# A decoder layer on one core: the third MLP weight block's cast and the four residual scalings are queued behind the last conversions of the MLP's input

## The chip, the cores and the metric

One core of one Trainium2 chip runs the kernel as a single program. The metric is the time of one execution on the device in microseconds (us). Engines are named as in the profile: PE is the tensor engine (PEld its weight loads), ACT the scalar engine, DVE the vector engine, POOL the GpSimd engine, and SP the engine whose queue issues most loads. All weights and activations are float32.

## The reference, cut to what matters

The layer mixes tokens by two branches (causal pooling and a state-space scan), merges them through gates and `w_o`, and then runs a squared-ReLU MLP. The part around the change is the end of the mixing and the start of the MLP:

```python
h = h + (gate_pool * y_pool + gate_ssd * y_ssd) @ w_o[i]
v = rmsnorm(h, mlp_norm_w[i])            # the kernel does this for the 512 tokens that are kept
hid = jax.nn.relu(v @ w_ff1[i])          # 1024 -> 4096
h = h + (hid * hid) @ w_ff2[i]           # 4096 -> 1024
out = rmsnorm(h, final_norm_w)           # the 16 meta tokens are dropped
```

## The kernel before, in words

Each float32 operand of a product is split into a high half, rounded to the type float32r (`vh`, `whi`, `hh`), and a low half, which is the rest (`vl`, `wlo`, `hl`). A product is then three PE products: high by high, low by high, high by low. ACT makes the high half by a cast, and DVE makes the low half by a subtraction that needs the high half. So each weight block of 128x1024 costs a load, one ACT cast and one DVE subtraction, and PE waits for both.

**Weights.** `block()` takes a block's tiles, loads `raw` over SP's queue (`block_load`, L85) and splits it (`block_split`: the cast on L93, the subtraction on L95). There are three `raw` buffers, used in turn: the load of a block waits until the block three places earlier has been cast and subtracted. `whi` and `wlo` have four buffers each. In this stretch the blocks are, by the numbers that the built program gives them: `raw_6687` and `raw_6728` (MLP columns 0 and 1), `raw_6810` and `raw_6843` (columns 2 and 3, the second pair), `raw_6885` and `raw_6918` (columns 4 and 5), `raw_7025` and `raw_7094` (columns 6 and 7). `raw_6918` takes the buffer of `raw_6810`. SP's queue also loads quarters of `w_ff2` and sums of them (`quarter`, L1195: tiles `b` and `t`). POOL loads and stores such sums through a queue of its own at the same time.

**The MLP's input.** The residual `ht` has four tiles of 128 tokens by 1024 channels. PE transposes it in four pieces (`turn`, L1085) into the PSUM banks `ptA`, `ptB`, `ptC` and `ptD`; `turned` (L1089 to L1100) makes from each piece four `vh` on ACT (L1094) and four `vl` on DVE (L1095), and from `ptA` and `ptD` also four plain copies `vf` on ACT (L1099). `ptD` is the last piece. The norm's factor is not applied to `v`: squares of `ht` are summed on ACT (L1077) into `ssum`, DVE makes `m2` from it (L1392 and L1393), and ACT multiplies the four tiles of `ht` by `m2` (L1397), so that all is in the same scale when the MLP's output is added.

**The MLP.** `ff1_plain(n)` multiplies two blocks (columns 2n and 2n+1) with `vh` and `vl` into PSUM banks `pf`, and ACT applies ReLU and the square (L1217 and L1218). For a pair of columns, `left_factors` (L1331 to L1349) makes the operands of the second product, which runs as Strassen-like products of sums of quarters: ACT casts `hh` (L1338 for three segments, L1348 for the other four), DVE subtracts `hl` (L1339, L1349) and makes the sums (L1344 to L1347). `sums_of_v` makes sums of quarters of `v` for later first products (DVE L1263 to L1275, ACT L1274). The second products accumulate in the PSUM tile `alpha` (`prod`, L1359 and L1362); after each, DVE adds it to `ht` (`onto`, L1066), and the next product accumulates into the same `alpha`, so it waits until that addition has read it.

**The order.** Each engine has a queue of its own and works in the order of its queue; an instruction that waits for a semaphore holds all behind it on its engine. The order on each engine comes from a scheduler, which the program may bind with `tc.issue_after(x)`: what is issued inside stands behind `x` on `x`'s engine. Pools of buffers and PSUM banks give the other dependences.

Of the kernel before, what the change touches and what calls it, by code (L numbers as in the profile page):

```python
# [11 lines left out]
AF = mybir.ActivationFunctionType  # L12
# [22 lines left out]
V_MIX, V_BG, V_PS, V_CW, V_CB, V_DS, V_SN, V_MN, V_DTB, V_AL = (  # L35
    0, 8, 24, 32, 160, 192, 208, 224, 232, 233)
# [27 lines left out]
def kernel(ctx: ExitStack, tc, xT, x, w, f1, f2, vec, fnw, out):  # L64
    nc = tc.nc
    act, dve, pe, pool = nc.scalar, nc.vector, nc.tensor, nc.gpsimd
# [10 lines left out]
    def block_tiles():  # L77
        b = nblk[0]
        nblk[0] += 1
        return (b, wp.tile([P, 1024], F32, tag="raw", name=f"raw{b}", bufs=3),  # L80
                wp.tile([P, 1024], F32R, tag="whi", name=f"whi{b}"),
                wp.tile([P, 1024], F32R, tag="wlo", name=f"wlo{b}"))

    def block_load(t, c):
        nc.sync.dma_start(t[1][:, c], w[t[0], :, c])  # L85

    def block_part(t, c):
        block_load(t, c)
        block_split(t, c)

    def block_split(t, c, behind=None):
        b, raw, hi, lo = t
        act.copy(hi[:, c], raw[:, c])  # L93
        with tc.issue_after(behind.ins) if behind is not None else nullcontext():
            dve.tensor_tensor(lo[:, c], raw[:, c], hi[:, c].bitcast(F32), op=ALU.subtract)  # L95

    def block(behind=None):
        t = block_tiles()
        block_load(t, slice(0, 1024))
        block_split(t, slice(0, 1024), behind)  # L100
        return t[2:]
# [48 lines left out]
    def col(off, i, n=P):  # L150
        return vs[:n, off + i : off + i + 1]
# [21 lines left out]
    def psum1(name):  # L173
        return psb.tile([P, 512], F32, tag="s", name=name)
# [151 lines left out]
    for i in range(2):  # L326
        pb = psum1(f"pb1_{i}")
        c = slice(3 * i, 3 * i + 3)
# [35 lines left out]
    for c in (slice(0, P), slice(P, W)):  # L364
        n = c.stop - c.start
# [634 lines left out]
    first = []  # L1000
    for n, d in enumerate(MERGE):
# [10 lines left out]
        wh, wl = block()  # L1012
# [13 lines left out]
    ht = hp_.tile([P, 4, D], F32, name="ht")  # L1026
# [14 lines left out]
    vh = [yp.tile([P, SEQ], F32R, tag="yh", name=f"vh{k}") for k in range(NK)]  # L1041
# [32 lines left out]
    def square_sums(T, half):  # L1074
        cs = slice(half * 512, (half + 1) * 512)
        for t in (2 * T, 2 * T + 1):
            act.activation(junk, ht[:, t, cs], AF.Square, accum_out=ssum[:, t, half : half + 1])  # L1077

    def turn(pts, T, half, ts=(0, 1)):

        for kk in range(4):
            k = 4 * half + kk
            for t in ts:
                o = (kk % 2) * 256 + t * P
                pe.transpose(pts[kk // 2][:, o : o + P], ht[:, 2 * T + t, k * P : (k + 1) * P], ident)  # L1085

    low_end = [None]

    def turned(pts, T, half):  # L1089
        for kk in range(4):  # L1090
            k = 4 * half + kk
            src = pts[kk // 2][:, (kk % 2) * 256 : (kk % 2) * 256 + 256]
            o = slice(256 * T, 256 * T + 256)
            act.activation(vh[k][:, o], src, AF.Copy, scale=col(V_MN, k))  # L1094
            low_end[0] = dve.scalar_tensor_tensor(vl[k][:, o], src, col(V_MN, k), vh[k][:, o].bitcast(F32),  # L1095
                                                  op0=ALU.mult, op1=ALU.subtract)
        for kk in range(0 if half else 4):
            k = 4 * half + kk
            act.activation(v32[k][:, o], pts[kk // 2][:, (kk % 2) * 256 : (kk % 2) * 256 + 256], AF.Copy,  # L1099
                           scale=col(V_MN, k))  # L1100
# [31 lines left out]
    turn(pt, 0, 0)  # L1132
    onto(1, 1, alpha, SUB)
    turned(pt, 0, 0)
    square_sums(0, 0)
    t4 = wo_split("b11")
    wo_prod(q5, "S4", s4, False, True)
    pp = psum2("ptB")
    pt = [pp[:, :512], pp[:, 512:]]
    turn(pt, 1, 1)  # L1140
    turned(pt, 1, 1)
    for t in range(2):
        onto(0, 1, q5[t], ADD, t)
    wo_prod(av, "A22", t4, False, True, (0,))
    onto(1, 0, av[0], ADD, 0)
    pt = banks("ptC")
    turn(pt, 0, 1)
    turned(pt, 0, 1)
    second_half = low_end[0]
    wo_prod(av, "A22", t4, False, True, (1,))  # L1150
# [2 lines left out]
    turn(ptD, 1, 0, (0,))  # L1153


    def ff1_begin(c, f):
        wh, wl = block()
        return psum1(f"pf{c}_{f}"), wh, wl

    def ff1_part(p, ks, first, last):  # L1160
        ps, wh, wl = p
        cs = [slice(k * P, (k + 1) * P) for k in ks]
        mm3s(ps, [((wh[:, c], wl[:, c]), (vh[k], vl[k])) for c, k in zip(cs, ks)], first, last)

    pf = [ff1_begin(0, 0)]
    ff1_part(pf[0], range(4, 8), True, False)
    turn(ptD, 1, 0, (1,))
    turned(ptD, 1, 0)
    for q in ((1, 1), (0, 1), (1, 0)):
        square_sums(*q)  # L1170
    pf.append(ff1_begin(0, 1))
    ff1_part(pf[1], range(4, 8), True, False)
    for p in pf:
# [9 lines left out]
    m2 = fa.tile([P, 4], F32, name="m2")  # L1183
# [14 lines left out]
    def pair_tile(n):  # L1198

        return tmp.tile([P, 4, 256], F32, tag="relu", name=f"r{n}")  # L1200
# [3 lines left out]
    def ff1_plain(n, parts=(range(NK),)):  # L1204
        r = pair_tile(n)
        for i in range(2):
            if pf:
                ps = pf.pop(0)[0]
            else:
                p = ff1_begin(n, i)  # L1210
                ps = p[0]
                for ks in parts if i else (range(NK),):
                    ff1_part(p, ks, ks[0] == 0, ks[-1] == NK - 1)
                    if ks[-1] < NK - 1 or not i:
                        yield
            ri = flat4(r[:, 2 * i : 2 * i + 2, :])
            act.activation(ri, ps, AF.Relu)  # L1217
            act.activation(ri, ri, AF.Square)  # L1218
        left_factors(n, r)
        yield  # L1220
# [110 lines left out]
    def left_factors(n, r):  # L1331

        c, p = divmod(n, 2)
        if p == 0:
            hids[c] = [hid.tile([P, 2, 7, 256], F32R, tag=t, name=f"{t}{c}") for t in ("hh", "hl")]
        hh, hl = (t[:, p] for t in hids[c])
        m = 4 if c == NC - 1 else 3
        act.copy(hh[:, :m, :], r[:, :m, :])  # L1338
        dve.tensor_tensor(hl[:, :m, :], r[:, :m, :], hh[:, :m, :].bitcast(F32), op=ALU.subtract)  # L1339
        if c == NC - 1:  # L1340
            return
        q = [r[:, i, :] for i in range(4)]

        dve.tensor_tensor(q[1], q[3], q[1], op=ALU.subtract)  # L1344
        dve.tensor_tensor(q[3], q[2], q[3], op=ALU.subtract)
        dve.tensor_tensor(q[2], q[1], q[2], op=ALU.subtract)
        dve.tensor_tensor(q[0], q[0], q[2], op=ALU.add)  # L1347
        act.copy(hh[:, 3:, :], r)  # L1348
        dve.tensor_tensor(hl[:, 3:, :], r, hh[:, 3:, :].bitcast(F32), op=ALU.subtract)  # L1349
# [39 lines left out]
    for n in range(3):  # L1389
        for _ in ff1_plain(n):  # L1390
            pass
# [2 lines left out]
    dve.tensor_tensor(be, m2, m2, op=ALU.mult)  # L1394
    dve.tensor_scalar(be, be, EPS, None, op0=ALU.mult)
    for t in range(4):
        act.activation(ht[:, t, :], ht[:, t, :], AF.Copy, scale=m2[:, t : t + 1])  # L1397

    sums_of_v(0)

    for c in range(NC - 1):
        z, e = c == 0, c == NC - 2

        n = 2 * c + 3
        a = ff1_plain(n, (range(4), range(4, NK))) if n < PLAIN else ff1_pair(n)
        b = ff1_pair(n + 1) if n + 1 < 16 else iter(())
        slots = [[a] * (1 if n < PLAIN else 2)] * 3 + [[a, b]] + [[b, b]] * 3
# [60 lines left out]
    c = NC - 1  # L1468
# [14 lines left out]
    for t in range(4):  # L1483
        T, st = t // 2, slice((t % 2) * P, (t % 2 + 1) * P)
        n = 0
        for half in range(2):
            parts = [(0, 512)] if half == 0 or t < 3 else [(0, 256), (256, 256)]
            for a, m in parts:
# [3 lines left out]
                i = 0  # L1492
# [4 lines left out]
                for k, seg in ((1, (A11, 3)[T]), (0, (A12, A22)[T])):  # L1497
                    wh, wl = wq[k, half]
                    for p in range(2):
                        x0 = p * 512 + a  # L1500
                        f = i == 0 and not (T == 0 and half == 0) and not a
# [5 lines left out]
                src = ps  # L1507
                if not a:
                    src = ht[:, t, cs]
# [146 lines left out]
```

## Time and profile before

| what | value |
|---|---|
| median of 3 runs | 1003.68 us (1002.7 to 1003.71) |
| the profiled execution, own time | 1003.18 us |
| its span | 1001.4 us |
| granted clock, mean | 0.999 |
| PE busy | 993.2 us (99%) |
| DVE busy | 793.2 us (79%) |
| ACT busy | 602.8 us (60%) |
| loads and stores | 171.47 MB, mean 171 GB/s |

The profiled execution spends 1.78 us outside of its span. Times in the views are microseconds from the span's start. A row of the timeline gives start, duration, engine, line, operation, output and inputs, the shape, how many instructions it merges, and in brackets how long the engine sat idle before it and what ended that. Durations overlap a little at the ends, since an engine begins an instruction while the one before drains.

### The profile page before, as it was taken

The numbers are of one execution on the slowest core, as the hardware profiler recorded it, in microseconds if no ns is written. First come the engines' busy times: TensorE is split into PE (matmuls) and PEld (weight loads), VectorE is DVE, ScalarE is ACT, GpSimd is POOL, SyncE is SP. The second block draws the span as 40 slices with busy tenths as digits, with TensorE's granted clock in tenths as the row PEclk, the third lists the DMA queues.
The fourth block names the chain that finished last, engine by engine and source line by source line (L and its number), as shares of the span: only waits on it lengthen the run. The fifth ranks groups of instructions, "written<-read, shape, count | busy, mean of one in ns | idle before, by whom it ended". The sixth has DMA issues, their size and how long they took to land.

```text
span 1001.4 us, 15539 instructions
## 1 busy us (share of the span) xinstructions
PE 993.2 (99%) x6095; PEld 878.3 (88%) x6095; DVE 793.2 (79%) x1147; ACT 602.8 (60%) x840; POOL 88.1 (9%) x148
## 2 busy tenths in 40 slices
PE   9999999999999999999999999999999999999997
PEld 7889898999889998988998888888889999999986
DVE  7988797979736687979789667876988888888885
ACT  8675958595827439483255343368666656656654
POOL 0022101111002011002201001121100000000000
PEclk9999999999999999999999999999999999999999
DMA  7378763678238635417978632879654464454432
GB/s 242 92 281 226 202 185 117 193 188 234 63 104 253 164 99 160 132 38 213 280 203 234 230 105 71 238 194 303 182 189 148 149 189 149 146 187 150 127 105 85
DMA packets 56202, 171.47 MB, mean 171 GB/s; under 512 B 6400, under 2 KB 7744, under 8 KB 55104
## 3 DMA queue, kind: packets, MB, share of 16 engines
q1 hardware_dynamic: 36576, 105.86, 32.5%
q0 software_dynamic: 18832, 63.71, 24.3%
q8 instruction: 48, 0.79, 0.3%
q10 hardware_dynamic: 720, 0.91, 0.3%
q14 instruction: 26, 0.21, 0.1%
HBM read 161.90 MB, written 48.40 MB: 210 GB/s over the span
## 4 chain that ended last, share of the span: by engine, by line
PE 98%; DMA 1%; ACT 0%; DVE 0%; issue 0%; SPq 0%; ACTq 0%
PE px L191 12%; PE px L1291 8%; PE alpha L1359 6%; PE pz L191 6%; PE px L193 6%; PE px L1294 4%; PE alpha L1362 3%; PE pgp L191 3%; PE pz L193 3%; PE pgs L191 3%; PE py L556 2%; PE pso L127 2%; PE po L550 2%; PE wo_alpha L1053 1%; PE pso L128 1%; PE pso L130 1%
## 5 line engine op out<-in xcount | busy, mean ns | idle before, releaser
L93 ACT CAST whi<-raw 128x1024 fp32r<-128x1024 f32 (+2 forms) x98 | 98.5, 1014 | 105.7 <-PE px L193 33.2
L95 DVE TENSOR_TENSOR wlo<-raw,whi 128x1024 fp32r<-128x1024 f32 (+2 forms) x98 | 114.7, 1176 | 50.9 <-ACT whi L93 33.1
L191 PE MATMUL px<-uh,whi 128*128 128x264 f32 (+1 forms) x448 | 113.2, 291 | 0.0
L193 PE MATMUL px<-ul,whi 128*128 128x264 f32 (+1 forms) x448 | 110.5, 285 | 0.0
L191 PEld LDWEIGHTS px<-uh,whi 128*128 128x128 f32 x448 | 84.6, 189 | 1.8 <-issue 1.4
L193 PEld LDWEIGHTS px<-ul,whi 128*128 128x128 f32 x448 | 84.3, 188 | 0.4 <-issue 0.2
L1066 DVE TENSOR_TENSOR ht<-ht,alpha 128x1024 f32<-128x1024 f32 x35 | 42.7, 1219 | 29.1 <-PE alpha L1359 29.1
L989 ACT CAST shi<-rawf 128x1024 fp32r<-128x1024 f32 x42 | 44.2, 1051 | 28.7 <-PE alpha L1362 18.2
L191 PE MATMUL px<-uh,wlo 128*128 128x264 f32 (+1 forms) x448 | 58.5, 283 | 0.0
L191 PEld LDWEIGHTS px<-uh,wlo 128*128 128x128 f32 x448 | 55.9, 188 | 0.0
L1359 PE MATMUL alpha<-shi,hh 128*128 128x512 f32 x140 | 55.2, 394 | 0.0
L1362 PE MATMUL alpha<-shi,hl 128*128 128x512 f32 x140 | 54.7, 391 | 0.0
L990 DVE TENSOR_TENSOR slo<-rawf,shi 128x1024 fp32r<-128x1024 f32 x42 | 51.2, 1218 | 0.6 <-ACT shi L989 0.6
L1294 PE MATMUL px<-vsl,shi 128*128 128x256 f32 x192 | 47.4, 280 | 0.0
L1291 PE MATMUL px<-vsh,shi 128*128 128x256 f32 x192 | 47.4, 281 | 0.0
L193 PE MATMUL pz<-ul,whi 128*128 128x512 f32 x112 | 43.6, 390 | 0.0
L191 PE MATMUL pz<-uh,whi 128*128 128x512 f32 x112 | 43.6, 389 | 0.0
L577 DVE RECIPROCAL rs<-rs 128x128 f32<-128x128 f32 x32 | 27.2, 909 | 13.9 <-ACT rs L575 13.8
L1359 PE MATMUL alpha<-slo,hh 128*128 128x512 f32 x140 | 37.4, 389 | 0.0
L1291 PEld LDWEIGHTS px<-vsh,shi 128*128 128x128 f32 x192 | 36.2, 188 | 0.9
L1294 PEld LDWEIGHTS px<-vsl,shi 128*128 128x128 f32 x192 | 36.1, 188 | 0.9
L1294 PE MATMUL px<-vl,shi 128*128 128x256 f32 x144 | 36.1, 283 | 0.0
(558 smaller groups left out, 2859.1 us busy)
## 6 DMA issues: line engine op xcount, KB each, us to landing
raw<-in_w SPq DMA_DIRECT2D x104, 512.0 KB, 4.4
f_t<-in_f POOLq DMA_DIRECT2D x38, 512.0 KB, 6.7
f_s<-in_f POOLq DMA_DIRECT2D x26, 512.0 KB, 8.6
b<-in_f SPq DMA_DIRECT2D x21, 512.0 KB, 4.6
rawf<-in_f SPq DMA_DIRECT2D x36, 256.0 KB, 3.2
rawf<-f_t SPq DMA_DIRECT2D x36, 256.0 KB, 3.0
abc<-acs_d POOLq DMA_DIRECT2D x8, 1024.0 KB, 7.6
f_t<-f_t POOLq DMA_DIRECT2D x12, 512.0 KB, 4.4
```

Source lines behind the costliest of these rows:

```text
L93: act.copy(hi[:, c], raw[:, c])
L95: dve.tensor_tensor(lo[:, c], raw[:, c], hi[:, c].bitcast(F32), op=ALU.subtract)
L191: pe.matmul(o, wt, rhs[0][k][:, c], start=part == 0 and k == 0, stop=part == 1 and k == NK - 1)
L193: pe.matmul(o, wt, rhs[1][k][:, c], start=False, stop=False)
L577: dve.reciprocal(rs[:, ctok(c)], rs[:, ctok(c)])
L989: splits.append((act.copy(hi, src), dve.tensor_tensor(lo, src, hi.bitcast(F32), op=ALU.subtract)))
L990: dve.tensor_tensor(lo, src, hi.bitcast(F32), op=ALU.subtract)))
L1066: added[0] = dve.tensor_tensor(o, o, src, op=op)
L1291: pe.matmul(ps, m, f[k][0], start=start and not low and k == 0, stop=stop and low == 1 and k == 3, skip_group_check=True)
L1294: pe.matmul(ps, m, f[k][1], start=False, stop=False, skip_group_check=True)
L1359: pe.matmul(ps[t], hh[:, p, seg, st], m, start=bool(first and not low and p == 0), stop=bool(last and low and p == 1), skip_group_check=True)
L1362: pe.matmul(ps[t], hl[:, p, seg, st], m, start=False, stop=False, skip_group_check=True)
```

## The change

The last `vh` and the last `vl` instruction of the MLP's input are kept as a pair `all_halves`. The third block (columns 2, `raw_6810`, the first of the second pair) has its cast bound behind that last `vh` on ACT and its subtraction behind that last `vl` on DVE. The four scalings of `ht` are bound behind that last `vh` on ACT. Nothing is added or removed, and no data or size changes.

```diff
     def block_split(t, c, behind=None):
         b, raw, hi, lo = t
-        act.copy(hi[:, c], raw[:, c])
+        first, behind = behind if isinstance(behind, tuple) else (None, behind)
+        with tc.issue_after(first.ins) if first is not None else nullcontext():
+            act.copy(hi[:, c], raw[:, c])
...
-            act.activation(vh[k][:, o], src, AF.Copy, scale=col(V_MN, k))
+            high_end[0] = act.activation(vh[k][:, o], src, AF.Copy, scale=col(V_MN, k))
...
-    def ff1_begin(c, f):
-        wh, wl = block()
+    def ff1_begin(c, f, behind=None):
+        wh, wl = block(behind)
...
     turned(ptD, 1, 0)
+    all_halves = (high_end[0], low_end[0])
...
-                p = ff1_begin(n, i)
+
+                p = ff1_begin(n, i, all_halves if (n, i) == (1, 0) else None)
...
     for t in range(4):
-        act.activation(ht[:, t, :], ht[:, t, :], AF.Copy, scale=m2[:, t : t + 1])
+        with tc.issue_after(all_halves[0].ins):
+            act.activation(ht[:, t, :], ht[:, t, :], AF.Copy, scale=m2[:, t : t + 1])
```

The scheduler moves more than these instructions. Line numbers grow by 2 to 5 in the changed kernel. PE's order and POOL's order are the same in both kernels.

ACT's queue before, where the last piece of the input (`ptD`) is converted; `whi_6811` is the cast of the third block, `whi_6844` that of the fourth:

```order
L1094 ACTIVATE vh_6375<-ptB,vs 128x256
L93 CAST whi_6811<-raw_6810 128x1024
L1094 ACTIVATE vh_6375<-ptC_6651,vs 128x256
L93 CAST whi_6844<-raw_6843 128x1024
L1077 ACTIVATE m_3_120,ssum<-ht 128x512
L1094 ACTIVATE vh_6368<-ptD_6681,vs 128x256
L1094 ACTIVATE vh_6370<-ptD_6682,vs 128x256
L1094 ACTIVATE vh_6369<-ptD_6681,vs 128x256
L1094 ACTIVATE vh_6371<-ptD_6682,vs 128x256
L1397 ACTIVATE ht<-ht,m_6787 128x1024
L1099 ACTIVATE vf_6353<-ptD_6681,vs 128x256
```

The same place now:

```order
L1096 ACTIVATE vh_6375<-ptB,vs 128x256
L1096 ACTIVATE vh_6375<-ptC_6651,vs 128x256
L1079 ACTIVATE m_3_120,ssum<-ht 128x512
L1096 ACTIVATE vh_6368<-ptD_6681,vs 128x256
L1096 ACTIVATE vh_6370<-ptD_6682,vs 128x256
L1096 ACTIVATE vh_6369<-ptD_6681,vs 128x256
L1096 ACTIVATE vh_6371<-ptD_6682,vs 128x256
L95 CAST whi_6811<-raw_6810 128x1024
L1101 ACTIVATE vf_6353<-ptD_6681,vs 128x256
```

Both casts have moved behind the four `vh` of `ptD`, the third block's directly behind them and the fourth's behind the four `vf` that follow, and the scalings of `ht` have left this place.

ACT's queue before, some instructions later, where the blocks of columns 4 and 5 are cast (`whi_6886`, `whi_6919`) and the first pair of columns (`r_6794`) becomes `hh_6799`:

```order
L1397 ACTIVATE ht<-ht,m_6787 128x1024
L93 CAST whi_6886<-raw_6885 128x1024
L1217 ACTIVATE r_6794<-pf_0_6693 128x512
L1397 ACTIVATE ht<-ht,m_6787 128x1024
L1218 ACTIVATE r_6794<-r_6794 128x512
L1217 ACTIVATE r_6794<-pf_1_6734 128x512
L93 CAST whi_6919<-raw_6918 128x1024
L1218 ACTIVATE r_6794<-r_6794 128x512
L1397 ACTIVATE ht<-ht,m_6787 128x1024
L1338 CAST hh_6799<-r_6794 128x768
```

The same place now:

```order
L95 CAST whi_6844<-raw_6843 128x1024
L95 CAST whi_6886<-raw_6885 128x1024
L1221 ACTIVATE r_6794<-pf_0_6693 128x512
L1402 ACTIVATE ht<-ht,m_6787 128x1024
L1222 ACTIVATE r_6794<-r_6794 128x512
L95 CAST whi_6919<-raw_6918 128x1024
L1221 ACTIVATE r_6794<-pf_1_6734 128x512
L1402 ACTIVATE ht<-ht,m_6787 128x1024
L1222 ACTIVATE r_6794<-r_6794 128x512
L1402 ACTIVATE ht<-ht,m_6787 128x1024
L1342 CAST hh_6799<-r_6794 128x768
```

Behind the cast of `whi_6919` there stood a square and one scaling ahead of `hh_6799`; now a ReLU, a scaling, a square and another scaling stand there.

SP's queue before, with the loads of the stretch (`raw` blocks of the first product's weights, `b` and `t` of the second's):

```order
L85 DMA raw_6885<-in_w 128x1024
L1195 DMA b_0_6984<-in_f 128x1024
L1195 DMA t_0_7003<-f_t_870 128x1024
L85 DMA raw_6918<-in_w 128x1024
L85 DMA raw_7025<-in_w 128x1024
L1195 DMA b_0_7068<-in_f 128x1024
L1195 DMA b_0_7075<-in_f 128x1024
L85 DMA raw_7094<-in_w 128x1024
```

And now:

```order
L85 DMA raw_6885<-in_w 128x1024
L1198 DMA b_0_6984<-in_f 128x1024
L1198 DMA t_0_7003<-f_t_870 128x1024
L1198 DMA b_0_7068<-in_f 128x1024
L1198 DMA b_0_7075<-in_f 128x1024
L85 DMA raw_6918<-in_w 128x1024
L85 DMA raw_7025<-in_w 128x1024
L85 DMA raw_7094<-in_w 128x1024
```

The two `b` loads, which wait for no `raw` buffer, now stand ahead of the two `raw` loads.

More of the change, by code (lines that the diff above doesn't have):

```diff
@@ L1085, in turn @@
                 pe.transpose(pts[kk // 2][:, o : o + P], ht[:, 2 * T + t, k * P : (k + 1) * P], ident)
-    low_end = [None]
+    low_end, high_end = [None], [None]
     def turned(pts, T, half):
```

## The prediction

> **What bounds the kernel now.** I read the page's head first, then the waits of PE, then the windows of the stretch that the change touches.
>
> ```profile
> span 1001.4 us, 15539 instructions
> PE 993.2 (99%) x6095; PEld 878.3 (88%) x6095; DVE 793.2 (79%) x1147; ACT 602.8 (60%) x840; POOL 88.1 (9%) x148
> PE pdt L233 <- DVE ones_r L138: 1.5, 1, 1.5
> PE px L181 <- DVE xl L241: 0.6, 2, 0.3
> 655.00:720.00 65.00, 65.00 (x303) 53.92 (x302) 53.18 (x85) 49.63 (x85) 11.70 (x17) 1.00 0.88 249
> ```
>
> PE is the bound, and its only two waits, 2.1 us together, are at the start. In the window around the change (columns: PE, PEld, DVE, ACT, POOL, clock, DMA share, GB/s) PE works for 65 of 65 us at full clock. So an earlier conversion of the MLP's input has no PE wait to remove. The change can only cost, by making something late that is now in time; the question is how wide the margins are on ACT, DVE and the loads, which are nearly full here as well.
>
> **The change part by part.** First the conversions themselves and the third block's cast, from the timelines of ACT, DVE and PE.
>
> ```profile
> 673.10 1.08 ACT L93 CAST whi<-raw 128x1024 fp32r<-128x1024 f32 x1
> 677.72 0.82 ACT L1094 ACTIVATE vh<-ptD,vs 128x256 fp32r<-128x256 f32 x2
> 679.56 0.86 ACT L1094 ACTIVATE vh<-ptD,vs 128x256 fp32r<-128x256 f32 x2 [1.02 <-DVE vl L1095]
> 675.00 1.22 DVE L95 TENSOR_TENSOR wlo<-raw,whi 128x1024 fp32r<-128x1024 f32 x1
> 677.22 1.23 DVE L95 TENSOR_TENSOR wlo<-raw,whi 128x1024 fp32r<-128x1024 f32 x1 [1.01 <-ACT whi L93]
> 685.65 0.39 PE L127 MATMUL pf<-vh,whi 128*128 128x512 f32 x1
> ```
>
> The two subtractions at 675.00 and 677.22 leave DVE's way, so the 1.02 us for which ACT waited in the middle of its four `vh` should go. The last `vh` ended at 679.56 + 0.86 = 680.4. It can now end between 677.72 + 0.82 + 0.86 = 679.4 and 680.4; the path to PE gains nothing by it. The third block's cast follows with 1.05 us and its subtraction with 1.22 us: whi at about 681.2, wlo at about 682.0 (bounds 681.7 and 682.7). PE wants that block at 685.65, so the move of the cast itself is covered by 4 us and costs nothing. The fourth block's cast comes behind four `vf` and is wanted a whole product later still: nothing either.
>
> What the move does cost hangs on the buffer. The load of column 5's block (`raw_6918`) takes the third block's buffer, so it waits for that subtraction. SP's timeline, and the time from issue to landing of the loads in it, one by one (t, raw, raw, b, both b, raw):
>
> ```profile
> 673.31 0.33 SPq L1195 DMA_DIRECT2D t<-f_t  x1
> 676.28 2.52 SPq L85 DMA_DIRECT2D raw<-in_w  x2
> 678.85 1.02 SPq L1195 DMA_DIRECT2D b<-in_f  x2
> 686.18 0.33 SPq L85 DMA_DIRECT2D raw<-in_w  x1
> t<-f_t SPq DMA_DIRECT2D x1, 512.0 KB, 8.6
> raw<-in_w SPq DMA_DIRECT2D x1, 512.0 KB, 8.8
> raw<-in_w SPq DMA_DIRECT2D x1, 512.0 KB, 10.4
> b<-in_f SPq DMA_DIRECT2D x1, 512.0 KB, 12.2
> DMA to landing us min/median/max: 12.2/13.0/13.8
> raw<-in_w SPq DMA_DIRECT2D x1, 512.0 KB, 8.3
> q1 hardware_dynamic: 1578, 5.23, 50.6%
> q0 software_dynamic: 935, 3.37, 50.5%
> ```
>
> The last two rows are the queues from 668.5 to 695: SP's loads (q1) and POOL's (q0) fill the 16 engines between them. The load was issued at 676.28, right behind the subtraction that ended at 675.00 + 1.22. Now it goes out at about 682.0, 5.7 us later, and behind both `b` loads, which no longer wait. In the old order the queue landed one block after the other: raw at 676.28 + 8.8 = 685.1, raw at (676.28 + 2.52 − 0.33) + 10.4 = 688.9, b at 678.85 + 12.2 = 691.1, the other b at 679.4 + 13.8 = 693.2, raw at 686.18 + 8.3 = 694.5. All are 512 KB and the queue is never empty, so I give the same places to the new order: b, b, **column 5's block at 691.1**, column 6's at 693.2, column 7's at 694.5. The bounds are the page's median for such loads from 682.0 (first row of the next fence), 686.4, and the longest of this stretch, 682.0 + 13.8 = 695.8. I take 691.1, since 9.1 us is what the loads here take.
>
> [...]
>
> The cast of column 5's block stands in ACT's queue, and all behind it waits for the load.
>
> ```profile
> raw<-in_w SPq DMA_DIRECT2D x104, 512.0 KB, 4.4
> 686.82 0.62 ACT L1217 ACTIVATE r<-pf 128x512 f32<-128x512 f32 x1
> 687.29 1.08 ACT L93 CAST whi<-raw 128x1024 fp32r<-128x1024 f32 x1
> 688.23 0.67 ACT L1218 ACTIVATE r<-r 128x512 f32<-128x512 f32 x1
> 688.76 1.18 ACT L1397 ACTIVATE ht<-ht,m 128x1024 f32<-128x1024 f32 x1
> 688.40 1.23 DVE L95 TENSOR_TENSOR wlo<-raw,whi 128x1024 fp32r<-128x1024 f32 x1 [2.25 <-ACT whi L93]
> 690.69 0.96 DVE L1339 TENSOR_TENSOR hl<-r,hh 128x768 fp32r<-128x768 f32 x1 [1.06 <-ACT hh L1338]
> 696.58 1.23 DVE L1349 TENSOR_TENSOR hl<-r,hh 128x1024 fp32r<-128x1024 f32 x1 [1.12 <-ACT hh L1348]
> 701.97 0.39 PE L127 MATMUL pf<-vh,whi 128*128 128x512 f32 x1
> ```
>
> The cast moves from 687.29 to 691.1: **+3.8 us**. PE wants this block only at 701.97, so it is in time itself. What is late is DVE: its subtraction ends at 693.4 instead of 688.40 + 1.23 = 689.6. Then DVE waits for `hh`. Before, a square and one scaling stood between; now a ReLU (0.62) and a second scaling (1.18) too, about 1.6 us more after their overlaps, so DVE's wait of 1.06 us becomes 2.7. In return the later wait of 1.12 us goes, since by then ACT is ahead of the four small sums that DVE must do first. Net **+0.5 us**, with bounds of 0 (both hidden) and 1.6 (nothing given back).
>
> From there to the point that matters, one window of DVE, and where PE meets it.
>
> ```profile
> 689.63:724.10 34.47, 31.96 (x51) 1.00 0.76 209
> 724.10 1.22 DVE L1066 TENSOR_TENSOR ht<-ht,alpha 128x1024 f32<-128x1024 f32 x1
> 710.95 1.21 DVE L1066 TENSOR_TENSOR ht<-ht,alpha 128x1024 f32<-128x1024 f32 x1
> 715.37 1.21 DVE L95 TENSOR_TENSOR wlo<-raw,whi 128x1024 fp32r<-128x1024 f32 x1
> 720.10 1.07 PE L130 MATMUL pf<-vh,wlo 128*128 128x512 f32 x4
> 726.45 0.39 PE L1359 MATMUL alpha<-shi,hh 128*128 128x512 f32 x1
> ```
>
> DVE works for 31.96 of these 34.47 us, in 51 instructions that stay the same 51. Of the 2.5 us of idle time 2.2 are the two waits just counted, so DVE can't catch up and carries 3.8 + 0.5 = 4.3 us to its addition of `alpha` at 724.10, which then ends at 725.32 + 4.3 = 729.6. PE's next product into `alpha` started at 726.45, 1.13 us behind that addition. So PE waits for 4.3 − 1.1 = **3.2 us**. Part of it may show earlier, at 720.10, where PE wants a `wlo` that was ready at 716.6 and now is ready at 720.9; that is 0.8 of the same 3.2, since a late PE then meets a DVE that is as late as before. All later work follows PE.
>
> Of the scalings alone: all four are wanted by the first addition of `alpha` to `ht`, at 710.95; they are done by about 697 (six ACT instructions of 0.6 to 1.2 us behind the late cast), so their own lateness costs nothing beyond the second one counted above.
>
> The sum: 1003.18 + 3.2 = 1006.4 against the profiled execution. The median of the runs stands 0.5 above that execution, so I predict **1006.9 us**.
>
> **The rivals.**
>
> *The load isn't held up* (not slower). If SP's block comes as fast as the kernel's median, it lands at 686.4, ahead of the old cast. What counts is the lateness that DVE's margin of 1.1 us takes: below a landing of about 687.29 + 1.1 − 0.5 = 687.9 nothing reaches PE, and the time is 1003.7, or up to 0.5 more if the reordering alone gives 1.6. For it: the two `b` loads go out right behind `t` at 673.31 and may be through sooner than I think. Against it: full engines until 694.5. Chance 0.18. [...]
>
> *The load comes as late as the `b` loads did.* After 13.8 us, at 695.8, it is 4.7 us beyond my place for it, and PE pays all of that: 3.2 + 4.7 = 7.9, so 1011.6. Anything from about 693.3 on counts here. Then the first product into `alpha` would wait for `hh` as well. For it: the `b` loads took that in the same queue. Against it: they were issued behind two loads that waited there, which my block is not. Chance 0.12.
>
> *Faster.* The conversions of `ptD` end up to 1 us sooner. That pays only if other executions have a wait there that this profile lacks; the runs lie 1.0 us apart, so 1.0 us is the most that I could find for it: 1002.7. Chance 0.04.
>
> **How the numbers follow.** The forecast, a landing between about 688 and 693.3, has the remaining 0.66; its own range is 1004 to 1009. About 0.2% or 2.0 us is what a measurement of this kernel can tell from no change. The forecast stays under that if the block lands before 689.9, which I give 0.06 of the 0.66; slower by more is then 0.60 + 0.12 = 0.72. Faster by more than 0.2% needs twice what I could find for it: 0.02. The rest, 0.18 + 0.06 + 0.02 = 0.26, is within. The range 1003.4 to 1009.2 leaves out most of the late case, the faster one, and a little of the case in which nothing happens: its lower edge lies just under 1003.7.
>
> **What would show it.** In the changed kernel's timelines: the third block's cast at about 680 directly behind the last `vh`; the load of column 5's block issued at about 682 and landing near 691; ACT idle for several us with a release by that load; DVE's wait for `hh` grown to 2 to 3 us; PE waiting for DVE at `alpha` (and perhaps at a `wlo` before it), in total about 3.2 us, near 720 to 727, and nowhere else. The prediction is wrong if the load lands before 688, if DVE catches up before its addition of `alpha`, or if PE shows no wait there while the time is longer.

## The result, and the profile after

The changed kernel takes 1007.81 us (median of 6 runs, 1006.37 to 1008.98), the kernel before beside it 1003.54 us (6 runs, 1002.7 to 1004.44). The ratio is 1.0040, with a 95% interval of 1.0029 to 1.0051: slower by 4.3 us. The forecast was 1006.9 us, range 1003.4 to 1009.2.

The profiled execution took 1008.98 us with a span of 1007.2 us, so it is 5.8 us longer than the profiled execution before (span 1001.4 us). It is the longest of the six runs, and the medians lie 4.3 us apart. The decomposition below is of those 5.8 us.

The head of the page of after, PE's waits (columns: us in total, times, the longest), three windows of after, and the first of these windows of the kernel before (columns: PE, PEld, DVE, ACT, POOL busy, granted clock, DMA share, GB/s):

```profile
span 1007.2 us, 15537 instructions
PE 995.1 (99%) x6095; PEld 879.2 (87%) x6095; DVE 793.7 (79%) x1147; ACT 602.7 (60%) x840; POOL 88.2 (9%) x148
```

```profile
PE alpha L1363 <- DVE ht L1068: 2.2, 1, 2.2
PE pf L132 <- DVE wlo L97: 2.0, 1, 2.0
```

```profile
655.00:740.00 85.00, 80.83 (x372) 66.55 (x371) 66.01 (x103) 56.92 (x96) 11.69 (x17) 0.98 0.78 219
732.15:735.56 3.41, 3.41 (x11) 2.73 (x10) 2.65 (x4) 2.12 (x3) 0.00 (x0) 0.50 0.86 275
735.56:740.00 4.44, 4.44 (x29) 3.95 (x28) 3.67 (x7) 1.45 (x3) 0.00 (x0) 1.00 0.66 194
```

```profile
655.00:740.00 85.00, 85.00 (x410) 71.13 (x409) 71.18 (x108) 60.75 (x100) 11.70 (x17) 1.00 0.79 224
```

The work is the same 6095 matmuls, but PE now has two waits that the kernel before does not have, 1.99 and 2.17 us. In the 85 us around the change it is idle for 85.00 − 80.83 = 4.17 us, which is their sum. There is a second loss that no busy share shows: for 3.41 us behind the second wait the granted clock is 0.50, so PE does half the work there and loses about 1.7 us. The start times agree: PE's order is the same in both kernels, the first matmul behind the second wait starts 4.37 us later than before (730.82 against 726.45), and the one that stood at 729.64 before starts 6.05 us later (735.69). 4.2 + 1.7 = 5.9 us, which accounts for the 5.8 us.

Now the path, from the load to PE, in the timelines of after (start, duration, engine, line, operation, in brackets the idle time before it and what ended it). First SP's queue, and the time from issue to landing of the first of the three `raw` loads, column 5's:

```profile
673.41 0.91 SPq L1198 DMA_DIRECT2D b<-in_f  x2
681.27 4.07 SPq L85 DMA_DIRECT2D raw<-in_w  x3
```

```profile
raw<-in_w SPq DMA_DIRECT2D x1, 512.0 KB, 10.6
```

Both `b` loads now go out more than 7 us ahead of column 5's load, which is issued at 681.27, when the third block's late subtraction has released its buffer. It lands at 681.27 + 10.6 = 691.9.

ACT, where the last conversions and the third block's cast stand, and where column 5's cast stands:

```profile
678.19 0.87 ACT L1096 ACTIVATE vh<-ptD,vs 128x256 fp32r<-128x256 f32 x2 [0.19 <-DVE vl L1097]
678.96 1.04 ACT L95 CAST whi<-raw 128x1024 fp32r<-128x1024 f32 x1
691.93 1.05 ACT L95 CAST whi<-raw 128x1024 fp32r<-128x1024 f32 x1 [6.53 <-DMA raw<-in_w]
695.97 0.82 ACT L1342 CAST hh<-r 128x768 fp32r<-128x768 f32 x1
```

The last `vh` ends at 679.06, 1.4 us sooner than before, and the third block's cast stands directly behind it. Then ACT sits idle for 6.53 us in front of column 5's cast, and `r` and `hh`, which need nothing of that load, stand behind it.

DVE gets both waits from ACT and carries them to its addition of `alpha`; PE meets them there:

```profile
693.01 1.22 DVE L97 TENSOR_TENSOR wlo<-raw,whi 128x1024 fp32r<-128x1024 f32 x1 [8.02 <-ACT whi L95]
696.83 0.96 DVE L1343 TENSOR_TENSOR hl<-r,hh 128x768 fp32r<-128x768 f32 x1 [2.59 <-ACT hh L1342]
720.72 1.22 DVE L97 TENSOR_TENSOR wlo<-raw,whi 128x1024 fp32r<-128x1024 f32 x1
729.46 1.21 DVE L1068 TENSOR_TENSOR ht<-ht,alpha 128x1024 f32<-128x1024 f32 x1
```

```profile
722.00 1.20 PE L132 MATMUL pf<-vh,wlo 128*128 128x512 f32 x4 [1.99 <-DVE wlo L97]
730.82 0.47 PE L1363 MATMUL alpha<-shi,hh 128*128 128x512 f32 x1 [2.17 <-DVE ht L1068]
732.38 0.63 PE L1363 MATMUL alpha<-shi,hh 128*128 128x512 f32 x1
```

The lateness against the kernel before is 4.64 us at the cast (691.93 against 687.29), 4.61 at its subtraction (693.01 against 688.40) and 5.36 at the addition (729.46 against 724.10). 35 us of DVE's queue lie between, and nothing of it is made up. On the way the subtraction at 720.72 ends at 721.94, and PE, waiting for that `wlo`, goes on at 722.00; the addition ends at 730.67, and PE goes on at 730.82. The last PE row lasts 0.63 instead of 0.39 us, inside the stretch of half clock.

### The profile page after: what moved, and what is told of

It reads as the page before. It is cut to its first block, busy times and chain, and to the rows that moved or that the text cites. A ratio compares the mean times of both kernels' runs of the same rounds, so it can differ in the third digit from the quotient of the medians.

```text
span 1007.2 us, 15537 instructions
## 1 busy us (share of the span) xinstructions
PE 995.1 (99%) x6095; PEld 879.2 (87%) x6095; DVE 793.7 (79%) x1147; ACT 602.7 (60%) x840; POOL 88.2 (9%) x148
## 4 chain that ended last, share of the span: by engine, by line
PE 93%; DVE 3%; DMA 1%; ACT 1%; issue 0%; SPq 0%; DVEq 0%; ACTq 0%
PE px L193 12%; PE px L1295 8%; PE alpha L1363 6%; PE pz L193 6%; PE px L195 6%; PE px L1298 4%; PE alpha L1366 3%; PE pgp L193 3%; PE pz L195 3%; PE pgs L193 3%; PE py L558 2%; PE pso L129 2%; PE po L552 2%; PE wo_alpha L1055 1%; PE pso L130 1%; PE pgp L195 1%
## 5 line engine op out<-in xcount | busy, mean ns | idle before, releaser
L1295 PE MATMUL px<-vh,shi 128*128 128x256 f32 x144 | 36.3, 284 | 0.0
```

What stands on the lines that cost most here:

```text
L1295: pe.matmul(ps, m, f[k][0], start=start and not low and k == 0, stop=stop and low == 1 and k == 3, skip_group_check=True)
```

## The experiments

The theory under test: column 5's load loses its place in SP's queue, its cast holds ACT, DVE carries that, PE waits. Against it stand these. The loss could be the buffer that comes free 5 us later, whatever the place. It could be the scalings, or the new order on ACT and DVE, rather than the load. And the two PE waits may explain only 4.2 of the 5.8 us if the clock's loss belongs to something else.

The kernel before ran beside these in three groups; its medians were 1003.26 (23 runs), 1003.35 (7) and 1003.25 us (21).

**1. The casts alone.** The other half needs no run: with only the scalings bound, the built order is the one of before on every engine, because they stood behind the last `vh` already. In the changed kernel they move only since the casts beside them do. So this run takes their binding away from the changed kernel:

```diff
     for t in range(4):
-        with tc.issue_after(all_halves[0].ins):
-            act.activation(ht[:, t, :], ht[:, t, :], AF.Copy, scale=m2[:, t : t + 1])
+        act.activation(ht[:, t, :], ht[:, t, :], AF.Copy, scale=m2[:, t : t + 1])
```

> The change without its second half: the third block's cast is bound behind the last conversion, the four scalings are free again (they then stand around the conversions, and behind the cast of column 5's block only one scaling and the ReLU stand ahead of hh). Theory (column 5's load comes late and holds ACT, DVE carries the lateness to its addition of alpha): the load still goes out at about 682 and lands near 691 to 692; only the 1.2 us scaling behind it goes, so PE's two waits shrink from 4.2 us in all to about 3, and the time is about 1006 to 1007. Rival (the moved ACT work, scalings and ReLU, is the cost): the time falls to 1003.5 to 1004.

Measured: 1006.0 us (6 runs, 1004.34 to 1008.44), ratio 1.0029 (1.0015 to 1.0042). PE's waits and ACT's timeline of this kernel:

```profile
PE alpha L1363 <- DVE ht L1068: 1.8, 1, 1.8
```

```profile
690.63 1.05 ACT L95 CAST whi<-raw 128x1024 fp32r<-128x1024 f32 x1 [3.85 <-DMA raw<-in_w]
```

The load goes out at 683.21 and lands at 690.6. The cast is 3.34 us late and the addition of `alpha` 3.25 us (727.35). The time is in the range expected, but by one wait of 1.8 us and not by two of about 3 us together. So the bound casts alone cost 2.7 us of the 4.3, and here the new order on DVE adds nothing to the load's lateness. In the full change the scalings come late as well: `hh` stands behind one more of them, DVE waits 2.59 us for it instead of 1.07, and lateness grows by 0.75 us on the way to the addition. The rest goes with the load, which landed 1.3 us later there although it was issued 1.9 us sooner.

**2. The place in the queue, given back.** The changed kernel, with the two `b` loads bound behind column 5's load on SP. The buffer still comes free only at 681. One of the two `b` loads now stands between column 5's and column 6's load. The order on PE, ACT, DVE and POOL is that of the changed kernel.

```diff
+        loads.append(nc.sync.dma_start(t[1][:, c], w[t[0], :, c]))
...
+    column5 = loads[-1]
...
+                with tc.issue_after(column5.ins) if c == 0 and n in ("b22", "b21") else nullcontext():
+                    raws[n] = quarter(f"{n}_{c}", f2[c, q[n]] if n in q else wsum["f2", c, n])
```

> The changed kernel, with the two b loads bound behind column 5's load on SP's queue, as they stood before; the third raw buffer still comes free at about 681. Theory: with only t's load ahead of it (landing near 683) column 5's block lands at 685 to 688 instead of 691.9, the lateness is within DVE's margin of 1.1 us or a little over it, and the time is 1003.5 to 1004.5. Rival (the buffer's 5 us are the cost, not the queue): it lands at 681 + 10 as now, time 1006 to 1008. Rival (the reordering on ACT): 1005 to 1007, with the load early.

Measured: 1004.25 us (11 runs, 1002.63 to 1007.3), ratio 1.0010 (1.0001 to 1.0018). SP's timeline, the load's time to landing, ACT's timeline and PE's waits:

```profile
681.09 0.33 SPq L87 DMA_DIRECT2D raw<-in_w  x1
```

```profile
raw<-in_w SPq DMA_DIRECT2D x1, 512.0 KB, 6.4
```

```profile
687.57 1.05 ACT L97 CAST whi<-raw 128x1024 fp32r<-128x1024 f32 x1 [2.36 <-DMA raw<-in_w]
```

```profile
PE alpha L1365 <- DVE ht L1070: 0.3, 1, 0.3
```

The load goes out as late as in the changed kernel (681.09 against 681.27), lands after 6.4 instead of 10.6 us, and the cast is 0.28 us late instead of 4.64. DVE's wait for `hh` is still 2.59 us, and the addition is 1.0 us late (725.10), of which PE feels 0.3. So 3.3 of the 4.3 us hang on the place in the queue, and what is left, 1.0 us, is the late buffer and the order on ACT together.

**3. The place in the queue, taken from the kernel before.** The kernel before, with the four loads of `w_ff2` issued first and column 5's load bound behind the last of them. The order on all other engines is that of before, and the buffer comes free as early as before.

```diff
+        with tc.issue_after(quarter_loads["b21"].ins) if t[0] == column5 else nullcontext():
+            nc.sync.dma_start(t[1][:, c], w[t[0], :, c])
...
+    early = {n: quarter(f"{n}_0", wsum["f2", 0, n] if n == "t1" else f2[0, q])
+             for n, q in (("b11", B11), ("t1", None), ("b22", B22), ("b21", B21))}
+    column5 = nblk[0] + 3
...
+        raws = {} if c else early
```

> The kernel before with one thing of the change: on SP's queue the four w_ff2 loads (b, t, b, b) stand ahead of column 5's load, as in the changed kernel; ACT, DVE, PE and POOL have the order of before, and the third raw buffer comes free at 676 as before. Theory by places in the queue: column 5's block lands third of the five, at 690 to 692 as in the changed kernel, the cast is 3 to 4.6 us late, and with only the old single scaling behind it PE waits 2 to 3.5 us: 1005.5 to 1007.5. Rival (duration from issue counts, the buffer is what matters): it lands at 676.3 + 9 = 685 to 687, no cost, 1003.5.

Measured: 1006.26 us (6 runs, 1004.92 to 1008.16), ratio 1.0028 (1.0016 to 1.0039). SP, landing, ACT and PE's waits:

```profile
676.79 0.33 SPq L89 DMA_DIRECT2D raw<-in_w  x1
```

```profile
raw<-in_w SPq DMA_DIRECT2D x1, 512.0 KB, 14.1
```

```profile
690.87 1.05 ACT L97 CAST whi<-raw 128x1024 fp32r<-128x1024 f32 x1 [2.85 <-DMA raw<-in_w]
```

```profile
PE alpha L1363 <- DVE ht L1070: 1.8, 1, 1.8
```

Issued 0.5 us later than before, the load lands 5.8 us later, at 690.9, and 3.0 of the 4.3 us are back with no instruction moved on ACT, DVE or PE. The late buffer is not needed for it. The place in the queue alone makes the load late. Six kernels side by side say the same. In the kernel before and in experiment 2 column 5's load stands ahead of both `b` loads: it was issued at 676.28 and 681.09 and landed at 685.1 and 687.5. In the four in which it stands behind them (after, experiments 1, 3 and 4) it was issued between 676.8 and 683.2 and landed between 690.6 and 693.3.

**4. The cast behind the work that it held.** The changed kernel, with column 5's cast bound behind the first `hh` on ACT and its subtraction behind the first `hl` on DVE; the load stays late.

```diff
+        factor_end.append((act.copy(hh[:, :m, :], r[:, :m, :]),
+                           dve.tensor_tensor(hl[:, :m, :], r[:, :m, :], hh[:, :m, :].bitcast(F32), op=ALU.subtract)))
...
-                p = ff1_begin(n, i, all_halves if (n, i) == (1, 0) else None)
+                p = ff1_begin(n, i, all_halves if (n, i) == (1, 0) else factor_end[0] if (n, i) == (2, 1) else None)
```

> The changed kernel, with the cast of column 5's block bound behind the first hh on ACT and its subtraction behind the first hl on DVE: the load stays as late as it is (issued at 681, landing near 691.9), but ACT and DVE don't wait for it with the first pair's factors in hand. Theory: DVE gets hl at about 691 instead of 697, PE wants the block at 702 and gets it, no wait on PE, 1003.5 to 1004.2. Rival (the late block itself is wanted by PE, or the loads behind it are late): PE waits for wlo as now, 1006 to 1008.

Measured: 1003.66 us (11 runs, 1002.95 to 1005.78), ratio 1.0003 (0.9994 to 1.0012). ACT's timeline and PE's waits:

```profile
690.09 0.85 ACT L1343 CAST hh<-r 128x768 fp32r<-128x768 f32 x1
693.27 1.05 ACT L95 CAST whi<-raw 128x1024 fp32r<-128x1024 f32 x1 [2.33 <-DMA raw<-in_w]
```

```profile
PE alpha L1364 <- DVE ht L1068: 1.8, 2, 1.0
```

The load lands at 693.3, later than in any other kernel here, and by the median the loss is gone but for 0.4 us, which the interval cannot tell from nothing. `hh` no longer waits for the load: its cast starts at 690.09, ahead of column 5's, against 695.97 in the changed kernel. So by the median the late load costs through what stands behind its cast.

The traced execution is less clear. It is the longest of the 11 runs (1005.78 us). DVE's subtraction of the block still waits 2.43 us for the cast there, the addition of `alpha` is 2.6 us late (726.70), and PE has 1.8 us of waits in two pieces, where none was expected. When the load landed in the shorter runs isn't known. The scheduler also moved more than the guard: four matmuls (`px`) stand earlier on PE, and several later instructions change places on ACT and DVE. How much of the recovery is theirs was not tested.

**5. Both remedies.** The changed kernel with the edits of 2 and 4 together.

> The changed kernel with both remedies: the two b loads behind column 5's load, and the cast of column 5's block behind the first factors. Theory: no PE wait is left, 1003.2 to 1003.8, as the kernel before; the input's conversions, which end 1 us sooner than before, still bring nothing. Rival (a gain of the earlier conversions was hidden by the load's cost): under 1002.5.

Measured: 1003.38 us (11 runs, 1002.28 to 1005.85), ratio 1.0000 (0.9991 to 1.0009). PE has no wait in the stretch, and the addition of `alpha` stands at 724.11, where it stood before (724.10). ACT's timeline at the last conversions:

```profile
678.44 0.87 ACT L1098 ACTIVATE vh<-ptD,vs 128x256 fp32r<-128x256 f32 x2 [0.18 <-DVE vl L1099]
679.21 1.04 ACT L97 CAST whi<-raw 128x1024 fp32r<-128x1024 f32 x1
```

The last `vh` ends at 679.3, 1.1 us sooner than before, with all the loss taken away, and the kernel is no faster than before. So no gain of the earlier conversions was hidden under the loss. The scheduler moved the same four matmuls on PE, and other instructions on ACT and DVE, as in 4.

**6. The kernel before, with the guard alone.** The edit of 4 in the kernel before: column 5's cast and subtraction behind the first `hh` and `hl`.

> The kernel before, with only the cast and subtraction of column 5's block bound behind the first hh and hl (a version meant to do without the risk: a load of that block that comes late in some execution no longer holds ACT). Theory: PE waits nowhere in the stretch in the profiled execution of the kernel before, so the median stays, 1003.0 to 1003.6; at most the longest of its executions (to 1006.3) get fewer, if those come from this load. Rival (the binding costs DVE's order something): 1004 to 1005.

Measured: 1003.27 us (11 runs, 1002.35 to 1004.07), ratio 1.0000 (0.9991 to 1.0009), with no PE wait in the stretch. Taking that cast out of the way brings nothing where its load is in time. Its longest run is 1004.07 us, where the kernel before reached 1006.33 us in one of 21 runs (and once in the 23 beside the first experiments); with so few long runs it is not shown that the guard is the reason.

**7. A PE wait by itself.** This measures what a wait at that place costs with the loads left alone. The kernel before gets k copies of `alpha` on DVE ahead of its second addition to `ht`, the one at 724.10, and PE's next products are bound behind so that PE meets the wait. A few later instructions change places on PE, ACT and DVE.

```diff
+                with tc.issue_after(prod_end[0].ins) if not c else nullcontext():
+                    next(run, None)
...
+        for _ in range(0 if c else 2):
+            dve.tensor_copy(alpha, alpha)
```

With k = 2:

> The kernel before, with two copies of the accumulator alpha onto itself on DVE ahead of its second addition to ht (values unchanged), and the MLP products that follow bound behind the product into alpha on PE, so that PE waits there: about 2 times 1.2 us, and the subtractions that the queue puts between, less DVE's margin of 1.1 us, 2 to 3 us in one wait. Theory A (a single wait of this size leaves the clock alone; it took two waits of 2 us within 11 us to halve it): the granted clock stays whole, and the time is 1003.3 plus the wait, 1005.3 to 1006.3. Theory B (one wait of over 2 us is enough): half clock for about 3.4 us behind it, 1.7 us more, 1007 to 1008.

With k = 4:

> The same with four copies: one wait of 4.5 to 6 us. Theory A and B both expect the clock to be halved behind a wait this long if waits halve it at all: 1003.3 plus the wait plus about 1.7 us, 1009 to 1011. If the clock stays whole here, the half clock of the changed kernel has another cause than PE's waits, and the time is 1008 to 1009.5.

Measured: k = 2, 1007.85 us (4 runs, 1006.0 to 1009.11), ratio 1.0044 (1.0027 to 1.0061); k = 4, 1012.41 us (4 runs, 1011.06 to 1013.35), ratio 1.0091 (1.0076 to 1.0107). PE's waits and windows of k = 2, then of k = 4:

```profile
PE alpha L1360 <- DVE ht L1066: 2.9, 1, 2.9
```

```profile
727.94:734.76 6.82, 5.95 (x16) 4.82 (x17) 4.36 (x7) 1.26 (x2) 0.00 (x0) 0.50 0.50 164
734.76:740.00 5.24, 5.24 (x33) 4.67 (x33) 4.26 (x5) 2.38 (x3) 0.00 (x0) 1.00 0.26 92
```

```profile
PE alpha L1360 <- DVE ht L1066: 6.3, 1, 6.3
```

```profile
729.35:739.59 10.24, 6.20 (x17) 5.12 (x18) 8.05 (x11) 2.10 (x2) 0.00 (x0) 0.50 0.32 103
```

One wait of 2.85 us puts 6.82 us of the span under half clock. PE works for 5.95 us of it and so loses 3.0 us: the wait costs about twice its length. The wait of 6.3 us has 6.20 us of work under half clock, 3.1 us lost. The sums, 2.9 + 3.0 = 5.9 and 6.3 + 3.1 = 9.4 us, stand over the measured 4.5 and 9.1 us of the medians; the spans of the profiled executions grew by 5.0 and 9.7 us. The matmul that starts at 729.64 in the kernel before starts at 734.86 (k = 2) and 739.50 (k = 4): since the wait PE has fallen back by another 2.9 us in both. So the expectation that a single wait of 2 to 3 us leaves the clock alone fell. With k = 4 the wait and the time came out over what was expected (4.5 to 6 us and 1009 to 1011 us), and in both the loss by the clock was not 1.7 us but 2.9.

## Why the prediction was right, by its own steps

*No gain is possible, since PE does not wait before.* Shown: the conversions end 1.1 to 1.4 us sooner in the changed kernel and in experiment 5, and neither is faster. The two rows of PE's waits hold three waits, not two; all stand at the start, so the step is not touched.

*The third block's cast directly behind the last `vh`, at about 680, at no cost.* It starts at 678.96, and no PE wait stands at its product.

*Column 5's load issued at 682.0, landing at 691.1 by its place in the queue.* It was issued at 681.27 and landed at 691.9. The step was right in kind: experiments 2 and 3 move the place with the buffer's time left alone, and the landing follows the place both times. The same 512 KB took 6.4 us (experiment 2), 8.8 (before), 10.6 (after) and 14.1 us (experiment 3) from issue to landing, so a duration added to the issue, which gave the lower bound of 686.4, is not how that number comes about in this stretch. The rival in which the load isn't held up fell with it, and so did the one that had it at 695.8.

*The cast +3.8 us.* It was +4.64, by the 0.8 us that the load was later than its forecast.

*DVE's wait for `hh` 2.7, the later one gone, net +0.5.* The wait was 2.59 us, and the later one of 1.12 us is gone (0.15 us is left, at a `slo` at 700.86). These two alone make +0.56 us; from the subtraction to the addition the lateness grew by 0.75 us.

*DVE carries it to the addition of `alpha`; PE's margin there is 1.13 us.* This can be read against five kernels. The lateness of the addition and PE's waits in the stretch were 1.00 and 0.3 us (experiment 2), 3.25 and 1.8 (experiment 1), 3.49 and 1.8 (experiment 3), 5.36 and 4.2 (after), and 0.01 and none (experiment 5). Lateness less 1.13 gives nothing, 2.1, 2.4, 4.2 and nothing. The margin is right within 0.6 us. For the single waits the rest is PE's own place: the last matmuls ahead of the addition start at 725.54 in the kernel before, and at 725.09, 725.82 and 726.08 in experiments 2, 1 and 3. Less this shift too, the waits come to 0.32, 1.84 and 1.82 us, against 0.30, 1.82 and 1.80 measured. The first wait of experiment 4 fits as well (2.60 us late, 725.99, so 1.02 against 1.01).

*PE waits 3.2 us, 0.8 of it at the `wlo` at 720.10.* It waits 4.2 us, and 1.99 of it at that `wlo`. The term was undersized by 1.0 us: 0.8 us from the landing and 0.25 from what DVE added.

*1003.18 + 3.2.* Here a term was left out. The prediction priced a PE wait at its length, and behind the second of two waits the clock was halved for 3.41 us, another 1.7 us. Experiment 7 shows half clock behind one wait by itself: 6.82 us of it behind a wait of 2.85 us, and 10.24 us behind one of 6.3 us. The single waits of 1.8 us in experiments 1 and 3 left the mean clock at 0.999 in their profiled executions, and at 0.998 or 0.999 in 4 and 3 of their six runs. In the others it was 0.997, as in the profiled execution of after (3.41 us at half clock are 0.0017 of its span), and these are the longest: 1008.44 and 1007.73 us in experiment 1, and 1008.16, 1007.07 and 1006.5 us in experiment 3. That fits a term which is on in some runs and off in others at the same wait, but those runs left no trace to show it. In all six runs of after the clock was 0.997 or 0.998. A mean of 0.998 alone decides nothing: the profiled executions of experiments 2 and 5 have it too, with 0.3 us of PE waits in this stretch and none.

In the profiled execution the two misses make 2.6 us (1008.98 against 1006.4). In the median they show as 0.9 us only (1007.81 against 1006.9), because the execution that was profiled is the longest here, where before it lay below the median. So the half us that the prediction added for the median did not carry over, and that the forecast came so close is in part luck: 1006.9 + 2.6 = 1009.5 would lie outside of its range.

What stays open is why every landing in SP's queue came 0.1 to 1.2 us later than the places of before gave (685.2 and 689.0 for the two `b` against 685.1 and 688.9, then 691.9, 694.4 and 695.6 against 691.1, 693.2 and 694.5). Between kernels the landing at one and the same place differs by up to 2.7 us (685.1 and 687.5, 690.6 to 693.3). POOL's queue shares the 16 DMA engines (from 668.5 to 695 in after its packets took 53.2% of their time, those of SP's queue 45.0%) and was not varied. Of the 4.3 us, the 1.0 us that experiment 2 leaves was not taken apart into the late buffer and the order on ACT.

## What to carry to other kernels

Before moving a cast, ask which buffer its last reader releases, which load waits for that buffer, and which loads in the same queue then overtake it: here, where the DMA engines were full (a share of 0.98 from 668.5 to 695 in after), that place moved the landing, and not the time of issue. Issued at 676.79 behind both `b` loads the block landed at 690.9 (experiment 3), and issued at 681.09 ahead of them at 687.5 (experiment 2). A cast that waits for a load belongs behind the work on its engine that doesn't need the load: bound there, the median came back to within 0.4 us of the kernel before, though the one traced execution, the longest, still had 1.8 us of PE waits. And on an engine that is the bound, don't price a wait at its length alone: behind waits of 2.17 us (after) and 2.85 us (k = 2) PE lost another 1.7 and 3.0 us under half clock.

## What the runs showed of the hardware

The stretches with a granted clock of 0.50 were 3.41 us (after), 6.82 us (k = 2) and 10.24 us (k = 4) long, that is one, two and three times 3.41 us. In k = 2 and k = 4 they begin while PE still waits (at 727.94 and 729.35, where PE goes on at 728.81 and 733.39), in after 1.33 us behind the wait (at 732.15, where PE goes on at 730.82). Inside them matmuls of 512 columns start 0.43 us apart, instead of 0.23 (726.45 and 726.68 in the kernel before). In k = 2:

```profile
728.81 0.77 PE L1360 MATMUL alpha<-shi,hh 128*128 128x512 f32 x1 [2.85 <-DVE ht L1066]
729.37 0.63 PE L1363 MATMUL alpha<-shi,hl 128*128 128x512 f32 x1
729.80 0.63 PE L1360 MATMUL alpha<-shi,hh 128*128 128x512 f32 x1
```

Not every wait went with half clock. The clock was 0.50 behind the single waits of 2.85 us (k = 2) and 6.3 us (k = 4), and behind the second wait of after, 2.17 us. Behind the first wait of after, 1.99 us up to 722.00, it was 1.00 until 732.15, and behind the single waits of 1.8 us in experiments 1 and 3 it was 1.00 too. The windows are those of after, of experiment 1, and of experiment 3 twice:

```profile
722.00:732.15 10.15, 7.98 (x34) 6.32 (x35) 9.89 (x14) 6.25 (x10) 0.00 (x0) 1.00 0.38 113
720.00:740.00 20.00, 18.04 (x96) 15.16 (x95) 19.25 (x26) 12.17 (x18) 0.00 (x0) 1.00 0.58 175
727.00:731.00 4.00, 2.20 (x10) 1.75 (x10) 4.00 (x5) 3.94 (x6) 0.00 (x0) 1.00 0.59 155
731.00:738.00 7.00, 6.87 (x43) 6.02 (x42) 6.55 (x10) 3.84 (x6) 0.00 (x0) 1.00 0.83 276
```

What tells these cases apart was not shown, nor whether the first wait of after had a part in the half clock behind the second.
